# Every two weight slabs get places of their own for hi and lo within 256 bytes, in a one-core hybrid decoder layer

## The chip, the cores and the metric

The kernel runs on one core of a Trainium2 chip. The metric is the device time of one execution in microseconds (us), as the median of several runs.

## What is computed

One layer of a decoder trunk in float32 over 256 tokens of width 2048. An input projection (2048 to 6152 columns) feeds a gated causal convolution (31 taps, 8 channel groups) and a four-head mLSTM; their outputs go through an output projection (2048 to 2048), then a gated feed-forward part (2048 to 2 x 5632, a three-tap convolution on the gate, 5632 to 2048), with RMS norms around them. Cut to what matters:

```python
hn = rmsnorm(x, norm_mix_g);  p = hn @ w_in + b_in
u  = silu(group_norm(causal_dwconv(p[a] * sigmoid(p[g]), conv_dw_w, conv_dw_b), 8, gn_g, gn_b))
q, k = silu(causal_dwconv(p[q, k]));  v, o, li, lf = p[v], sigmoid(p[o]), p[i], log_sigmoid(p[f])
hm = group_norm(mlstm_chunkwise(q, k, v, li, lf), 4, mlstm_hn_g) * o
x  = x + concat(u, hm) @ w_out
up = rmsnorm(x, norm_ffn_g) @ w_up
x  = x + (silu(causal_dwconv(up[:5632])) * up[5632:]) @ w_down
out = rmsnorm(x, norm_final_g)
```

## The kernel before

All weights come as slabs of two row blocks of 128: 128 partitions by two times `w` float32 columns (`w` is 512, or 344 in the o projection). There are 400 slabs, in the order in which they are used, and one loop over them issues everything, by hand (`manual_schedule`). In turn i of the loop the SP queue is told to load slab i+5 (`load`, lines 178 to 193), slab i+3 is split (`split`, lines 195 to 224), and the matmuls of slab i are issued. A split is a rounding to float32r on ScalarE (`hi`, line 219) and the difference `raw - hi` on VectorE, or for some slabs on GpSimd (`lo`, line 224). hi and lo have four buffers each (`SPLIT_BUFS`), raw five. The other operand of each product is also kept as a high and a low part, and a product is the sum of three float32r matmuls (hi by high, hi by low, lo by high).

The stages, and in which role hi and lo stand in each:

- a and g columns of w_in, then later q and k columns (`ws_group`, line 254): hi and lo are the stationary operand (the weights that TensorE loads), the moving operand is a block of 256 columns of `xp`. 64 slabs, 24 matmuls each, 1536 matmuls of 256 columns.
- o columns (`xs_group`, lines 298 to 300, `w` = 344): hi and lo are the moving operand, the weights are 128 columns of `xp`. 24 slabs, 288 matmuls of 344 columns. The second row block of a slab begins 344 x 4 = 1376 bytes behind the first, which is 96 more within 256.
- v columns (the same lines, `w` = 512): 16 slabs, 192 matmuls of 512 columns, weights from `xp`.
- output projection (the same lines): 32 slabs, 384 matmuls of 512 columns, weights from `mixh` and `mixl`.
- w_up (`wp_group`, lines 279 and 280): hi and lo are the weights; a matmul with hi moves 512 columns of `x1p` (which lies where `xp` lay), one with lo moves 256. 176 slabs, 1408 matmuls of each kind. This stage is the longest.
- w_down (lines 298 to 300 for three column blocks, lines 850 to 852 in `down_last` for the last): hi and lo move, the weights are from `ah` and `al`. 88 slabs, 792 + 240 matmuls of 512 columns and 48 of 256.

Where the tiles lie, in bytes of a partition, modulo 256, by the layout of the built kernel: every buffer of hi and of lo begins at 160 (the buffers are 4096 bytes apart), `xp` and `x1p` at 192, and `mixh`, `mixl`, `ah` and `al` at 160. All offsets inside them that the matmuls use are multiples of 512 bytes, except the 1376 of the o projection. So the place of a slab tile less the place of its partner, modulo 256, is 224 against `xp` and `x1p` (64 for the second row block in the o projection), and 0 against `mixh`, `mixl`, `ah` and `al`. This difference is called the **distance** below.

Besides, seven little arrays of constants (biases, taps, gains: `load_rows`, lines 110 to 118) are loaded as rows into seven buffers of 512 bytes (tag `rows`), turned by TensorE in `transpose_rows` (line 154) and copied out. They are loaded at the start (G) and in turns 1, 3 and 5, and turned at the start and in turns 10 and 12. `mlstm_scores` (line 574) writes one tile of tag `pw`, 384 columns, for each of four heads, into four buffers.

Of the kernel before, what the change touches and what calls it, by code (L numbers as in the profile page):

```python
# [9 lines left out]
F32 = mybir.dt.float32  # L10
F32R = mybir.dt.float32r
# [4 lines left out]
P = 128  # L16
# [15 lines left out]
W = 512  # L32

RAW_BUFS = 5
SPLIT_BUFS = 4
AHEAD = 3
SIG = 4
WARM = (6, 5)
BY_K = 3


@with_exitstack
def hybrid_layer_kernel(
# [7 lines left out]
    act, dve, pool, pe = nc.scalar, nc.vector, nc.gpsimd, nc.tensor  # L51
# [4 lines left out]
    slab = ctx.enter_context(tc.tile_pool(name="slab", bufs=1))  # L56
    ps = ctx.enter_context(tc.tile_pool(name="ps", bufs=1, space=PSUM))
    inner = ExitStack()
    mid = inner.enter_context(tc.tile_pool(name="mid", bufs=1))
# [3 lines left out]
    def mm_bank(name):  # L63
        return ps.tile([P, 512], F32, tag="mm", name=name, bufs=4)
# [42 lines left out]
    warm = cst.tile([P, 1], F32, tag="warm", name="warm")  # L107
    act.copy(warm, ones[:, 0:1])

    def load_rows(parts, name):  # L110
        n = sum(p[1] for p in parts)
        r = mid.tile([P, P], F32, tag="rows", name="rows_" + name, bufs=7)
        o = 0
        for ap, k in parts:
            nc.sync.dma_start(r[o:o + k, :], ap)
            o += k
        return r, n
# [4 lines left out]
    rows = {}  # L122
# [44 lines left out]
    slabs = []  # L167
# [5 lines left out]
        tasks[cur[0] + delay].append((fn, cost))  # L173

    raw_t, hi_t, lo_t = {}, {}, {}
    mid_hook = []

    def load(i):
# [5 lines left out]
        if len(s["src"].shape) == 4:  # L184
            d = d.rearrange("p (k s c) -> p k s c", k=s["nk"], s=2)
            for h in range(2):
                if i < BY_K:
                    nc.sync.dma_start(d[:, h], s["src"][:, h])
# [11 lines left out]
    def split_tiles(i):  # L200
        s = slabs[i]
        n = s["nk"] * s["w"]
        raw = raw_t.pop(i)
        hi = slab.tile([P, 2 * W], F32R, tag="hi", name=f"hi{i}", bufs=SPLIT_BUFS)
        lo = slab.tile([P, 2 * W], F32R, tag="lo", name=f"lo{i}", bufs=SPLIT_BUFS)
        s["eng"] = pool if s["pool"] and i >= 8 and i % 2 else dve
        hi_t[i] = hi[:, :n].rearrange("p (k c) -> p k c", k=s["nk"])
        lo_t[i] = lo[:, :n].rearrange("p (k c) -> p k c", k=s["nk"])
        s["lo"] = 0.0 if s["eng"] is pool else 1.1 * n + 30
        return raw, hi, lo  # L210
# [15 lines left out]
    def w_slab(wap, kt, nk, col, w, fn, on_pool):  # L226
        if col is None:
            src = wap(kt)
        else:
            src = wap[kt * P:(kt + nk) * P, col:col + w].rearrange("(k p) c -> p k c", p=P)  # L230
        slabs.append(dict(src=src, w=w, nk=nk, mm=fn, pool=on_pool))


    def ws_group(wap, col, mov, nk, done, on_pool):
        st = {}

        def mk(kt):
            def fn(hi, lo):
                if kt == 0:
                    st["b"] = [mm_bank("ws0"), mm_bank("ws1")]  # L240
                mh, ml = mov()
                for k in range(2):
                    if mid_hook and mid_hook[0][0] == k:
                        mid_hook.pop(0)[1]()
                    hh, hl, lh = (hi, mh), (hi, ml), (lo, mh)
                    i = cur[0]
                    if i >= NK // 2:
                        steps = [(ct, a) for ct in range(4) for a in (hh, hl, lh)]
                    else:
                        steps = [(ct, a) for a in ((hh, lh, hl) if i + k == 0 else (hh, hl, lh)) for ct in range(4)]  # L250
                    for ct, (w, m) in steps:
                        o = v2(st["b"][ct // 2])[:, ct % 2, :]
                        first = kt + k == 0 and ct % 2 == 0 and w is hi and m is mh
                        pe.matmul(o, w[:, k, ct * P:(ct + 1) * P], m[:, kt + k, :], start=first,  # L254
                                  stop=kt + k == nk - 1 and w is lo, skip_group_check=True)
                if kt + 2 == nk:
                    done(st["b"])
            return fn

        for kt in range(0, nk, 2):  # L260
            w_slab(wap, kt, 2, col, W, mk(kt), on_pool)
# [3 lines left out]
    def wp_group(wap, col, done, alloc):  # L265
        st = {}

        def mk(kt):
            def fn(hi, lo):
                if kt == 0:  # L270
                    st["b"] = alloc()
                mp = xT["p2"]
                for k in range(2):
                    first, last = kt + k == 0, kt + k == NK - 1
                    m2 = mp[:, kt + k, :, :].rearrange("p h t -> p (h t)")
                    for ct in range(4):
                        o = st["b"][ct]
                        cs = slice(ct * P, (ct + 1) * P)
                        pe.matmul(o, hi[:, k, cs], m2, start=first, stop=last, skip_group_check=True)  # L279
                        pe.matmul(o[:, 0:T], lo[:, k, cs], mp[:, kt + k, 0, :], start=False, stop=last, skip_group_check=True)  # L280
                if kt + 2 == NK:
                    done(st["b"])
            return fn

        for kt in range(0, NK, 2):
            w_slab(wap, kt, 2, col, W, mk(kt), False)
# [18 lines left out]
    def xs_group(wap, col, w, stat, nk, done, on_pool):  # L305
        st = {}
        for kt in range(0, nk, 2):
            xs_slab(wap, col, w, stat, kt, kt == 0, kt + 2 == nk, st, done, on_pool)
# [39 lines left out]
    def done_ag(p):  # L348
        def fn(banks):
            sg = []  # L350

            def ev():
                for k in range(2):
                    c = 2 * p + k
                    act.activation(up[c][:, upos:], v2(banks[0])[:, k, :], AF.Identity, bias=bi[:, c:c + 1])
                sg.append(t2k("sg"))
                for k in range(2):
                    c = 2 * p + k
                    act.activation(v2(sg[0])[:, k, :], v2(banks[1])[:, k, :], AF.Sigmoid, bias=bi[:, 8 + c:9 + c])

            def mul():
                for k in range(2):
                    c = 2 * p + k
                    dve.tensor_mul(up[c][:, upos:], up[c][:, upos:], v2(sg[0])[:, k, :])
                conv_pair(p)
            d0 = 5 if p == 0 else 1
            after(d0, lambda: scale_banks(banks), 1300)
            after(d0 + 1, ev)
            after(d0 + 2, mul, 700)
        return fn  # L370
# [110 lines left out]
    def done_o(b):  # L481
        def fn(banks):
            def ev():
                for tt in range(NT):
                    dve.scalar_tensor_tensor(og[:, tt, b * OW:(b + 1) * OW], banks[tt][:, :OW], norm["r"][:, tt:tt + 1],
                                             bb[:, 1024 + b * OW:1024 + (b + 1) * OW], op0=ALU.mult, op1=ALU.add)

            def sig():
                n = OW if b < 2 else DC - 2 * OW
                for tt in range(NT):  # L490
                    o = og[:, tt, b * OW:b * OW + n]
                    act.activation(o, o, AF.Sigmoid)
                if b == 2:
                    gates()
            after(1, ev, 900)
            after(SIG, sig)
        return fn
# [65 lines left out]
    pw = {}  # L563
# [324 lines left out]


    ag = w_in[:, 0:2 * DC].rearrange("(k p) (s c) -> p k s c", p=P, s=2)  # L890
    for j in range(4):
        ws_group(lambda kt, j=j: ag[:, kt:kt + 2, :, T * j:T * (j + 1)], None, get_xT, NK, done_ag(j), True)
    for b in range(3):
        xs_group(w_in, OFF_O + OW * b, OW, get_xT, NK, done_o(b), True)
    for half in range(2):
        ws_group(w_in, OFF_Q + 512 * half, get_xT, NK, done_qk(0, half), True)
        ws_group(w_in, OFF_K + 512 * half, get_xT, NK, done_qk(1, half), True)

    at = defaultdict(list)
    v_start = len(slabs)  # L900
    for hp in range(2):
        xs_group(w_in, OFF_V + 512 * hp, W, get_xT, NK, done_v(hp), True)
    at[v_start - 2] += [(0, 0), (1, 1)]
# [3 lines left out]
        return mixh, mixl  # L907

    p3_start = len(slabs)
    sts = [{}, {}, {}, {"cv": True}]  # L910
    for n0 in (0, 2):
        for half in range(2):
            for n in (n0, n0 + 1):
                for kt in range(8 * half, 8 * half + 8, 2):
                    xs_slab(w_out, 512 * n, W, get_mix, kt, kt == 0, kt == 14, sts[n], done_out(n), False)

    for j in range(NF // 4):
        wp_group(w_up, 512 * j, done_gate(j), gate_banks)
        wp_group(w_up, DFF + 512 * j, done_up(j), up_banks)
    for n in range(3):  # L920
        xs_group(w_down, 512 * n, W, lambda: (ffn["ah"], ffn["al"]), NF, done_down(n, 512 * n, W), False)
    down_last(3, 1536, W, SPLIT_BUFS)
# [124 lines left out]
    credit = 0.0  # L1047
    split_next = [BY_K]
    for i in range(len(slabs)):
# [20 lines left out]
        while bg and credit > 0:  # L1070
            name = bg[0][0].__name__
            if name == "tail" and not first:
                break
            fn, cost = bg.popleft()
# [37 lines left out]
```

## Time and profile before

| | us |
|---|---|
| median of 3 runs | 1131.5 (1130.9 to 1131.64) |
| the profiled execution, its own time | 1131.08 |
| its span in the profile | 1129.3 |
| TensorE busy in it | 1118.7 |
| VectorE / ScalarE / GpSimd busy | 746.0 / 578.9 / 131.6 |

The profile calls TensorE's matmuls PE and its weight loads PEld, VectorE DVE, ScalarE ACT, GpSimd POOL and the DMA-issuing SyncE SP. A line such as L254 is a line of the kernel. The ends of matmuls are modelled and they overlap, so the duration of one matmul is no price; how far apart two of them start is one. Starts are given to 0.01 us, so the pitch (start to start) is read over many matmuls.

### The profile page before, as it was taken

The page shows a single profiled execution, that of the slowest core. Times are in us where ns is not written, and L with a number is a line of the kernel's source. Part 1 is how long each engine was busy: PE and PEld are TensorE (multiplying, and loading weights), DVE is VectorE, ACT ScalarE, POOL GpSimd, SP SyncE. Part 2 cuts the span into 40 slices and gives each one's busy share as a digit, 9 for nine tenths or more (in the row PEclk, how much of TensorE's full clock was granted, in tenths as well). Part 3 has the DMA queues.
Part 4 walks back from the last instruction along what each step waited for, and adds up shares of the span by engine and source line. Part 5 has one row for each costly group of instructions (what it writes and reads, how often), then busy time and mean ns, then how long its engine had stood idle before and what let it go on. Part 6 is the DMA issues. An engine that isn't in the chain of part 4 may idle for free.

```text
span 1129.3 us, 16955 instructions
## 1 busy us (share of the span) xinstructions
PE 1118.7 (99%) x6506; PEld 994.4 (88%) x6506; DVE 746.0 (66%) x1139; ACT 578.9 (51%) x823; POOL 131.6 (12%) x100
## 2 busy tenths in 40 slices
PE   9999999999999999999999999999999999999997
PEld 9999999998888888888888888888888888888886
DVE  5498999986765557657666666676576645454543
ACT  5745476754545455555545555455555444343433
POOL 0443554534200000000000000000000000000000
PEclk9999999999999999999999999999999999999999
DMA  8864665565655666666666666666666666666662
GB/s 262 272 190 125 193 205 186 175 183 166 218 192 184 173 195 190 192 188 185 188 199 191 184 191 189 194 188 192 188 186 188 197 193 230 197 188 196 191 195 89
DMA packets 122681, 215.40 MB, mean 191 GB/s; under 512 B 7440, under 2 KB 33256, under 8 KB 122088
## 3 DMA queue, kind: packets, MB, share of 16 engines
q1 hardware_dynamic: 121048, 209.92, 61.8%
q10 hardware_dynamic: 1552, 4.39, 1.0%
q8 instruction: 51, 0.84, 0.3%
q14 instruction: 30, 0.25, 0.1%
HBM read 212.19 MB, written 2.10 MB: 190 GB/s over the span
## 4 chain that ended last, share of the span: by engine, by line
PE 95%; DVE 3%; ACT 1%; issue 1%; DMA 0%; ACTq 0%; POOLq 0%; POOL 0%
PE ws L254 16%; PE gate L279 14%; PE up L279 14%; PE xs L298 9%; PE xs L299 9%; PE xs L300 9%; PE up L280 8%; PE gate L280 8%; PE xs L852 2%; PE xs L850 2%; PE xs L851 2%; DVE conv L386 2%; DVE lo L224 1%; DMA xs<-in_x_dram 0%; PE xT L940 0%
## 5 line engine op out<-in xcount | busy, mean ns | idle before, releaser
L224 DVE TENSOR_TENSOR lo<-raw,hi 128x1024 fp32r<-128x1024 f32 (+2 forms) x355 | 434.6, 1225 | 326.6 <-ACT hi L219 325.5
L219 ACT CAST hi<-raw 128x1024 fp32r<-128x1024 f32 (+2 forms) x401 | 411.5, 1030 | 452.4 <-PE xs L300 152.5
L279 PE MATMUL gate<-x1p,hi 128*128 128x512 f32 x704 | 245.0, 390 | 0.0
L279 PE MATMUL up<-x1p,hi 128*128 128x512 f32 x704 | 244.5, 390 | 0.0
L280 PE MATMUL up<-x1p,lo 128*128 128x256 f32 x704 | 198.5, 282 | 0.0
L280 PE MATMUL gate<-x1p,lo 128*128 128x256 f32 x704 | 198.5, 282 | 0.0
L254 PE MATMUL ws<-xp,hi 128*128 128x256 f32 x1024 | 178.5, 282 | 0.0
L279 PEld LDWEIGHTS up<-x1p,hi 128*128 128x128 f32 x704 | 132.2, 188 | 27.7
L279 PEld LDWEIGHTS gate<-x1p,hi 128*128 128x128 f32 x704 | 132.2, 188 | 27.6
L254 PEld LDWEIGHTS ws<-xp,hi 128*128 128x128 f32 x1024 | 153.4, 189 | 0.8 <-issue 0.3
L254 PE MATMUL ws<-xp,lo 128*128 128x256 f32 x512 | 135.5, 280 | 0.5 <-DVE lo L224 0.5
L280 PEld LDWEIGHTS gate<-x1p,lo 128*128 128x128 f32 x704 | 133.1, 189 | 0.0
L280 PEld LDWEIGHTS up<-x1p,lo 128*128 128x128 f32 x704 | 133.1, 189 | 0.0
L224 POOL TENSOR_TENSOR lo<-raw,hi 128x1024 fp32r<-128x1024 f32 (+1 forms) x48 | 111.1, 2317 | 148.2 <-ACT hi L219 142.2
L299 PE MATMUL xs<-lo,ah 128*128 128x512 f32 x264 | 102.7, 389 | 0.0
L300 PE MATMUL xs<-hi,al 128*128 128x512 f32 x264 | 102.7, 389 | 0.0
L298 PE MATMUL xs<-hi,ah 128*128 128x512 f32 x264 | 102.7, 389 | 0.0
L386 DVE SCALAR_TENSOR_TENSOR conv<-up,cB,conv 128x256 f32<-128x256 f32 x240 | 97.6, 478 | 0.0
L254 PEld LDWEIGHTS ws<-xp,lo 128*128 128x128 f32 x512 | 93.2, 189 | 0.9 <-DVE lo L224 0.7
L827 POOL TENSOR_TENSOR rf<-ms,halves 128x1 f32<-128x1 f32 x2 | 1.1, 550 | 711.7 <-DVE ms L821 711.7
L300 PEld LDWEIGHTS xs<-hi,al 128*128 128x128 f32 x264 | 49.6, 188 | 10.4
L298 PEld LDWEIGHTS xs<-hi,ah 128*128 128x128 f32 x264 | 49.6, 188 | 10.4
(186 smaller groups left out, 1204.5 us busy)
## 6 DMA issues: line engine op xcount, KB each, us to landing
raw<-in_w_up_dram SPq DMA_DIRECT2D x176, 512.0 KB, 3.9
raw<-in_w_down_dram SPq DMA_DIRECT2D x88, 512.0 KB, 4.7
raw<-in_w_in_dram SPq DMA_DIRECT2D x48, 512.0 KB, 4.4
raw<-in_w_in_dram SPq DMA_DIRECT2D x64, 256.0 KB, 4.6
raw<-in_w_out_dram SPq DMA_DIRECT2D x32, 512.0 KB, 4.6
raw<-in_w_in_dram SPq DMA_DIRECT2D x24, 344.0 KB, 3.4
x<-in_x_dram ACTq DMA_DIRECT2D x2, 1024.0 KB, 7.7
xs<-in_x_dram SPq DMA_DIRECT2D x7, 256.0 KB, 5.6
```

The costliest lines, as they stand in the source:

```text
L219: copy(hi[:, c], raw[:, c])
L224: slabs[i]["eng"].tensor_sub(lo[:, c], raw[:, c], hi[:, c].bitcast(F32))
L254: pe.matmul(o, w[:, k, ct * P:(ct + 1) * P], m[:, kt + k, :], start=first, stop=kt + k == nk - 1 and w is lo, skip_group_check=True)
L279: pe.matmul(o, hi[:, k, cs], m2, start=first, stop=last, skip_group_check=True)
L280: pe.matmul(o[:, 0:T], lo[:, k, cs], mp[:, kt + k, 0, :], start=False, stop=last, skip_group_check=True)
L298: pe.matmul(o, sh[:, kt + k, ts_], hi[:, k, :w], start=first and k == 0, stop=False)
L299: pe.matmul(o, sh[:, kt + k, ts_], lo[:, k, :w], start=False, stop=False)
L300: pe.matmul(o, sl[:, kt + k, ts_], hi[:, k, :w], start=False, stop=last and k == 1)
L386: dve.scalar_tensor_tensor(a, up[c][:, t:t + T], cB[:, 8 * t + c:8 * t + c + 1], a, op0=ALU.mult, op1=ALU.add)
L850: pe.matmul(o, sh[:, kt, ts_], hi[:, k, c:c + cw], start=kt == first, stop=False, skip_group_check=True)
L851: pe.matmul(o, sh[:, kt, ts_], lo[:, k, c:c + cw], start=False, stop=False, skip_group_check=True)
L852: pe.matmul(o, sl[:, kt, ts_], hi[:, k, c:c + cw], start=False, stop=kt == NF - 1, skip_group_check=True)
```

## The change

Each buffer of hi and lo is made 256 bytes longer (`ROOM` = 64 columns), and the 1024 columns that are used begin at an offset inside it that depends on the slab. `places` gives it: a list of pairs for hi and lo is set per stage by `new_stage`, and every two slabs take the next pair. `BASE` = 224 is the distance of the buffers' own start from `xp`, so that the numbers in a list are distances from `xp`; where the partner is `mixh`, `mixl`, `ah` or `al`, 32 is taken off, and they are distances from these. The lists: `Q_WS` (a and g, q and k, w_down) has for hi all eight multiples of 32 and for lo the same plus 0, 64, 128 or 192; `Q_XS` (o, v, output projection) has the sixteen pairs of multiples of 64; `Q_FFN` (w_up) has all 64 pairs of multiples of 32 and then 24 pairs in which lo stands at 16, 144, 80 or 208. The stages take from them: a and g 16 pairs, q and k the other 16, o 12, v 8, output projection 16, w_up all 88, w_down 44. To make room the rows of constants no longer have seven buffers of their own: three of them at a time are slices of a tile of tag `pw`, three such tiles in all. Number, order, shape and engine of all instructions stay as they are. The sizes of all the tiles that move are multiples of 256, so the other tiles keep their places within 256.

```diff
--- before.py
+++ after.py
@@ -37,6 +37,8 @@
 SIG = 4
 WARM = (6, 5)
 BY_K = 3
+ROOM = 64
+BASE = 224
 
 
 @with_exitstack
@@ -107,9 +109,14 @@
     warm = cst.tile([P, 1], F32, tag="warm", name="warm")
     act.copy(warm, ones[:, 0:1])
 
+    row_tiles = []
+
     def load_rows(parts, name):
         n = sum(p[1] for p in parts)
-        r = mid.tile([P, P], F32, tag="rows", name="rows_" + name, bufs=7)
+        if not row_tiles:
+            t = mid.tile([P, 384], F32, tag="pw", name="rows_" + name, bufs=4)
+            row_tiles.extend(t[:, c * P:(c + 1) * P] for c in (2, 1, 0))
+        r = row_tiles.pop()
         o = 0
         for ap, k in parts:
             nc.sync.dma_start(r[o:o + k, :], ap)
@@ -173,6 +180,23 @@
         tasks[cur[0] + delay].append((fn, cost))
 
     raw_t, hi_t, lo_t = {}, {}, {}
+    stage = {}
+
+
+    def places():
+        n = (len(slabs) - stage["at"]) // 2
+        q = stage["q"]
+        h, l = q[n % len(q)]
+        return (h - BASE) % 256 // 4, (l - BASE) % 256 // 4
+
+    def new_stage(q):
+        stage["at"], stage["q"] = len(slabs), q
+
+    Q8 = [32 * a for a in range(8)]
+    Q_FFN = [(a, b) for a in Q8 for b in Q8] + [(a, b) for a in (64, 192, 0, 128, 32, 224) for b in (16, 144, 80, 208)]
+    Q_WS = [(a, (a + b) % 256) for b in (0, 64, 128, 192) for a in Q8]
+    Q_XS = [(a, b) for a in (0, 64, 128, 192) for b in (0, 64, 128, 192)]
+
     mid_hook = []
 
     def load(i):
@@ -201,8 +225,9 @@
         s = slabs[i]
         n = s["nk"] * s["w"]
         raw = raw_t.pop(i)
-        hi = slab.tile([P, 2 * W], F32R, tag="hi", name=f"hi{i}", bufs=SPLIT_BUFS)
-        lo = slab.tile([P, 2 * W], F32R, tag="lo", name=f"lo{i}", bufs=SPLIT_BUFS)
+        hi = slab.tile([P, 2 * W + ROOM], F32R, tag="hi", name=f"hi{i}", bufs=SPLIT_BUFS)
+        lo = slab.tile([P, 2 * W + ROOM], F32R, tag="lo", name=f"lo{i}", bufs=SPLIT_BUFS)
+        hi, lo = (t[:, o:o + 2 * W] for t, o in zip((hi, lo), s["at"]))
         s["eng"] = pool if s["pool"] and i >= 8 and i % 2 else dve
         hi_t[i] = hi[:, :n].rearrange("p (k c) -> p k c", k=s["nk"])
         lo_t[i] = lo[:, :n].rearrange("p (k c) -> p k c", k=s["nk"])
@@ -228,7 +253,7 @@
             src = wap(kt)
         else:
             src = wap[kt * P:(kt + nk) * P, col:col + w].rearrange("(k p) c -> p k c", p=P)
-        slabs.append(dict(src=src, w=w, nk=nk, mm=fn, pool=on_pool))
+        slabs.append(dict(src=src, w=w, nk=nk, mm=fn, pool=on_pool, at=places()))
 
 
     def ws_group(wap, col, mov, nk, done, on_pool):
@@ -888,16 +913,20 @@
 
 
     ag = w_in[:, 0:2 * DC].rearrange("(k p) (s c) -> p k s c", p=P, s=2)
+    new_stage(Q_WS)
     for j in range(4):
         ws_group(lambda kt, j=j: ag[:, kt:kt + 2, :, T * j:T * (j + 1)], None, get_xT, NK, done_ag(j), True)
+    new_stage(Q_XS)
     for b in range(3):
         xs_group(w_in, OFF_O + OW * b, OW, get_xT, NK, done_o(b), True)
+    new_stage(Q_WS[16:] + Q_WS[:16])
     for half in range(2):
         ws_group(w_in, OFF_Q + 512 * half, get_xT, NK, done_qk(0, half), True)
         ws_group(w_in, OFF_K + 512 * half, get_xT, NK, done_qk(1, half), True)
 
     at = defaultdict(list)
     v_start = len(slabs)
+    new_stage(Q_XS)
     for hp in range(2):
         xs_group(w_in, OFF_V + 512 * hp, W, get_xT, NK, done_v(hp), True)
     at[v_start - 2] += [(0, 0), (1, 1)]
@@ -907,6 +936,7 @@
         return mixh, mixl
 
     p3_start = len(slabs)
+    new_stage([(a - 32, b - 32) for a, b in Q_XS])
     sts = [{}, {}, {}, {"cv": True}]
     for n0 in (0, 2):
         for half in range(2):
@@ -914,9 +944,11 @@
                 for kt in range(8 * half, 8 * half + 8, 2):
                     xs_slab(w_out, 512 * n, W, get_mix, kt, kt == 0, kt == 14, sts[n], done_out(n), False)
 
+    new_stage(Q_FFN)
     for j in range(NF // 4):
         wp_group(w_up, 512 * j, done_gate(j), gate_banks)
         wp_group(w_up, DFF + 512 * j, done_up(j), up_banks)
+    new_stage([(a - 32, b - 32) for a, b in Q_WS])
     for n in range(3):
         xs_group(w_down, 512 * n, W, lambda: (ffn["ah"], ffn["al"]), NF, done_down(n, 512 * n, W), False)
     down_last(3, 1536, W, SPLIT_BUFS)
```

## Rows read from the trace of the kernel before

**Rows 1.** page, part 1: busy time and instructions; part 2: granted clock

```profile
PE 1118.7 (99%) x6506; PEld 994.4 (88%) x6506; DVE 746.0 (66%) x1139; ACT 578.9 (51%) x823; POOL 131.6 (12%) x100
...
PEclk9999999999999999999999999999999999999999
```

**Rows 2.** page, part 4: the chain, by engine

```profile
PE 95%; DVE 3%; ACT 1%; issue 1%; DMA 0%; ACTq 0%; POOLq 0%; POOL 0%
```

**Rows 3.** waits of TensorE: us in total, times, longest

```profile
PE warm L968 <- POOL ident masks.py:199: 1.4, 1, 1.4
...
PE xT L940 <- DMA xs<-in_x_dram: 0.5, 1, 0.5
...
PE ws L254 <- DVE lo L224: 0.5, 1, 0.5
...
PE xs L299 <- DVE lo L224: 0.4, 1, 0.4
```

**Rows 4.** chain in order of time, ws stages: start us, us, what

```profile
55.99 24.03 PE ws L254 x204
...
243.16 2.80 PE ws L254 x24
```

**Rows 5.** timeline of TensorE, o projection, first and last: start us, us, engine, line

```profile
118.06 0.32 PE L298 MATMUL xs<-hi,xp 128*128 128x344 f32 x1
...
142.41 0.32 PE L298 MATMUL xs<-hi,xp 128*128 128x344 f32 x1
```

**Rows 6.** timeline of TensorE, v projection, first and last

```profile
250.60 0.40 PE L298 MATMUL xs<-hi,xp 128*128 128x512 f32 x1
...
268.80 0.40 PE L298 MATMUL xs<-hi,xp 128*128 128x512 f32 x1
```

**Rows 7.** timeline of TensorE, w_up, first and last

```profile
500.07 0.39 PE L279 MATMUL gate<-x1p,hi 128*128 128x512 f32 x1
...
516.02 0.39 PE L279 MATMUL up<-x1p,hi 128*128 128x512 f32 x1
```

**Rows 8.** timeline of TensorE, output projection, first and last

```profile
360.05 0.39 PE L298 MATMUL xs<-hi,mixh 128*128 128x512 f32 x1
...
383.85 0.39 PE L298 MATMUL xs<-hi,mixh 128*128 128x512 f32 x1
```

**Rows 9.** timeline of TensorE, w_down, 512 columns and then 256

```profile
1100.04 0.39 PE L850 MATMUL xs<-hi,ah 128*128 128x512 f32 x1
...
1115.46 0.39 PE L852 MATMUL xs<-hi,al 128*128 128x512 f32 x1
...
1115.68 0.28 PE L850 MATMUL xs<-hi,ah 128*128 128x256 f32 x1
...
1118.56 0.28 PE L850 MATMUL xs<-hi,ah 128*128 128x256 f32 x1
```

**Rows 10.** chain in order of time, mLSTM scores, plain float32 passes

```profile
241.85 0.86 PE S L570 x4
```

**Rows 11.** busy time by stretch: us, PE, PEld, DVE, ACT, POOL, PEclk, DMA

```profile
150.00:200.00 50.00, 50.00 (x413) 48.51 (x414) 49.17 (x95) 35.19 (x49) 26.32 (x14) 1.00 0.60 190
...
500.00:600.00 100.00, 100.00 (x579) 88.67 (x578) 66.11 (x89) 52.26 (x77) 0.00 (x0) 1.00 0.66 190
...
600.00:700.00 100.00, 100.00 (x579) 88.63 (x578) 68.55 (x95) 54.22 (x81) 0.00 (x0) 1.00 0.66 190
```

**Rows 12.** groups by line and shape, the splits: busy us, mean ns, idle before

```profile
L224 DVE TENSOR_TENSOR lo<-raw,hi 128x1024 fp32r<-128x1024 f32 x337 | 417.3, 1239 | 322.3 <-ACT hi L219 321.3
...
L219 ACT CAST hi<-raw 128x1024 fp32r<-128x1024 f32 x373 | 391.1, 1051 | 434.9 <-PE xs L300 143.0 <-PE gate L279 114.9 <-PE up L279 91.2
```

**Rows 13.** rows of constants turned, scores written: ns, first and last start

```profile
L154 PE MATMUL tr<-ident,rows_G x1: 285/285/285, 2.9 to 2.9; 16*128 16x16 f32 x1
...
L154 PE MATMUL tr<-ident,rows_D x2: 237/240/242, 48.1 to 48.2; 88*128 88x88 f32 x2
...
L574 DVE SCALAR_TENSOR_TENSOR pw<-S,wt x4: 557/558/559, 243.2 to 285.2; 128x384 f32<-128x384 f32 x4
```

## The prediction, made before the change was run

> **What bounds the kernel now.** I read the page's first two parts first: TensorE is busy 1118.7 of 1129.3 us, and the granted clock is at its upper level, 2.4 GHz, throughout [rows 1]. The chain that ended last is 95% TensorE [rows 2], and all its waits for data together are 2.8 us, nearly half of that before the first product [rows 3]. So it is not starved: what it costs is how far apart its matmuls start. A busy TensorE says nothing about that, so I went on to the pitch, stage by stage, from long runs of matmuls without a break. Only pitches that lie on both sides of a change in roles or places can tell what this change does.
>
> A matmul of n columns that took one column per cycle at 2.4 GHz would take n / 2.4 ns. What a matmul takes beyond that I call its **extra**:
> - a, g, q and k: 24 matmuls in 2.80 us are 116.7 ns each against 106.7, so 10.0 extra; in an earlier stretch 204 in 24.03 us, 117.8 each, 11.1 extra [rows 4]. Distance 224, slab tiles are the weights. I take 10.5.
> - o: 156 starts from the first to the last row, 156.1 ns against 143.3: 12.8 [rows 5]. Distance 224 and 64 in turn, slab tiles move.
> - v: 78 starts, 233.3 against 213.3: 20.0 [rows 6]. Distance 224, slab tiles move.
> - w_up: 92 starts, 173.4 on the mean of 512 and 256 columns (160.0): 13.4 [rows 7]. Distance 224, slab tiles are the weights.
> - output projection: 105 starts, 226.7 against 213.3: 13.4 [rows 8]. Distance 0, slab tiles move.
> - w_down: 68 starts, 226.8, so 13.5; with 256 columns 24 starts, 120.0, so 13.3 [rows 9]. Distance 0, slab tiles move.
>
> Two things are to be seen. The extra is the same for 256 and for 512 columns at the same places [rows 9], so it is paid once a matmul and weight load, not per column. And it differs between v and w_down, which have the same shape, the same engine and the same role of the slab, by 6.5 ns [rows 6, 9]; what differs is the partner's tile and with it the distance. The plain float32 passes of the scores, 4 in 0.86 us, take 215 ns for 256 columns, twice the columns' time of the float32r ones (213.3) with 1.7 ns left over [rows 10]. So most of the extra is not a fixed price of a matmul either: where the moving operand is read at half the pace, it is gone. My reading is that weight load and moving operand get in each other's way in SBUF, and that it depends on where both stand. That other engines' traffic is not the cause: the splits run in bursts all through w_up, and two stretches with different DVE and ACT busy time hold the same 579 matmuls in 100 us [rows 11].
>
> In all the extra is 1536 x 10.5 + 288 x 12.8 + 192 x 20.0 + 2816 x 13.4 + 384 x 13.4 + 1080 x 13.5 ns = 16.1 + 3.7 + 3.8 + 37.7 + 5.1 + 14.6 = 81 us. This is all that a change of places can act on.
>
> **The change, part by part.** *The rows of constants.* G is turned at 2.9 us and the last two tiles by 48.2; the first score is written into a `pw` tile at 243.2 [rows 13]. No reader of a row comes within 190 us of the tile's next writer; the loads keep their order on SP and their bytes. If the loads of A and B1, which share G's tile, had to wait for G's turning, that lies before turn 1, in which the first of them is issued. Cost 0, with that cover; without it one of TensorE's turns would be late by a load, and nothing but `cA` to `cD` behind it.
>
> *The splits.* ScalarE and VectorE write to and read from shifted places, 373 casts of 1051 ns and 337 differences of 1239 ns, with 435 and 322 us of idle time ahead of them [rows 12]. If a place made them 10% slower (no row shows one that does), w_up's VectorE would go from 66% to about 70% busy [rows 11] and TensorE would not see it. The exception is q and k, where VectorE is busy 49.2 of 50 us [rows 11]: there 10% on some 25 splits, 3 us, would reach the end. I take 0, keep 0 to +3.
>
> *The pitch.* This is the sum. Distance is now scanned, so each stage gets the mean over its list instead of its one value. The rows show six readings, 10.5, 12.8, 20.0, 13.4, 13.4 and 13.5; their mean is 13.9. For a place that no row shows I take that mean, an estimate; its bounds are 10.0 and 20.0, the best and the worst reading.
> - a, g, q, k: from the best reading to the mean, 3.4 x 1536 = +5.2 us.
> - w_up: 0.5 x 2816 = +1.4 us.
> - v: its list has multiples of 64 only, and here 0 and 64 for hi, so the nearest rows are the 13.4 of distance 0 [rows 8]: -6.6 x 192 = -1.3 us.
> - o: in the new list as in the old one row block is a multiple of 64 away and the other is 32 off that: 0.
> - output projection +0.5 x 384 = +0.2, w_down +0.4 x 1080 = +0.4 us.
> - w_up's lo at 16, 144, 80 or 208: 24 pairs, so 48 slabs of 8 weight loads, 384 loads; bounds -3.4 to +6.6 ns each, -1.3 to +2.5 us; I take the middle, +0.6.
>
> Sum +6.5 us, on 1131.08 of the profiled execution (its span and 1.8 around it): 1137.6. The runs' median is 0.4 above the profiled one, so **1138**.
>
> *Bounds.* With every matmul at 10.0: -0.8 - 0.8 - 1.9 - 9.6 - 1.3 - 3.8 = -18 us. With all at 20.0: 14.6 + 2.1 + 0 + 18.6 + 2.5 + 7.0 = +45. A list that goes round all distances reaches neither end; the mean would have to lie a half of the way to the one (-9) or to the other (+22).
>
> The Trainium skill speaks against any effect: "TensorE: Matmul & The Clock Gate", section "Step-by-step: what each phase is for", says that the moving operand and the weight load have a read port each and that loading the next weights takes no bandwidth from the running matmul. "SBUF — State Buffer", section "Who interferes with whom", adds that PE never waits on anyone. By that the sum is 0 and the time 1131.5. The trace does not agree, with 233.3 against 226.8 ns for the same 512 columns.
>
> **The rivals.**
> - *The mean is better than the places before.* Distance 224 and 0, on which nearly all the time rests, were worse than the typical place. For it: v shows that a distance can cost 6.5 ns, so one may also save it, and the scores' 1.7 ns show that little is fixed. Against it: the largest stage sits at 13.4, under the mean of the readings, and a and g at the lowest. If the mean were 11.7, half way from 13.4 to 10.0: -1.7 x 2816 - 1.8 x 1080 - 1.7 x 384 + 1.2 x 1536 - 8.3 x 192 - 1.1 x 288 ns = -7.4 us, so 1124. In q and k a gain would be cut by VectorE.
> - *Places do not matter, roles do.* v would be slow because it takes its weights from `xp` and moves the slab, whatever the distance. Then nothing changes: 1131.5. For it: w_up holds the same 579 in both stretches [rows 11] though its tiles go round four buffers each; but these all have the same place within 256, so that is weak. Against it: o has the roles of v and 12.8 against 20.0; what differs, besides 344 columns, is that half of its distances are 64.
> - *Places in which both reads stay in step.* The slower end: weight loads that begin near the moving operand's place may be held over and over, as in v. The price is v's 20.0 or more. If every second place of all lists had it, and the others what their stage has now: half of the +45, 1154. It decides the result as soon as more than a tenth of the places are like v (+4.5). A time far above the forecast is this one.
> - *The shift does not do what it says*, because the period is not 256 bytes: with a shorter one of 64 or 128 some pairs repeat and the mean is taken over fewer places, the same forecast; with a longer one the 4352 bytes between buffers add places that no row shows. It widens the range, no more.
>
> **How the numbers follow.** The forecast, slower by a mean near that of the readings (1133.8 to about 1147), 0.50; in step, above that, 0.09; places do not matter, or the parts cancel (within 2.3 us), 0.16; the mean is better, 0.25. A measurement of this kernel can tell about 0.2% from no change, 2.3 us. So slower 0.59, same 0.16, faster 0.25. The range leaves out one in ten on either side: low end -9 us, a mean half way to the best reading, 1122; high end 1153, half way to the worst. The forecast's own part of it is 1134 to 1147.
>
> **What would show it.** The number of matmuls and their columns stay, so TensorE's pitch by pairs of slabs tells all: in w_up, 32 matmuls to two slabs at 13.4 extra are 5.55 us, and this should now change every two slabs, in steps that come back with the list. If all pairs take the same, places do not matter and the second rival is right. v should come down to about 227 ns a matmul; if it stays at 233, its role and not its distance makes it slow, and that step is wrong. a, g, q and k should rise above 117.8 ns. If waits of TensorE for hi or lo appear in q and k, the step on the splits was wrong; waits for rows of constants ahead of 50 us would make the first step wrong. If w_up's mean pitch falls under 173.4, the forecast's sign is wrong.

## The result and the profile after

The changed kernel takes **1141.17 us** (median of 3 runs, 1140.8 to 1141.5) against 1131.5: 9.7 us more, a ratio of 1.0087 with a 95% interval of 1.0064 to 1.011. The profiled execution has a time of its own of 1141.5 us and a span of 1139.8.

The page of the changed kernel, busy time and instructions, granted clock, and the first line of the chain:

```profile
PE 1128.5 (99%) x6506; PEld 992.1 (87%) x6506; DVE 741.7 (65%) x1139; ACT 578.7 (51%) x823; POOL 132.3 (12%) x100
...
PEclk9999999999999999999999999999999999999999
...
PE 93%; DMA 3%; DVE 1%; ACT 1%; issue 1%; SPq 1%; POOL 0%; ACTq 0%; POOLq 0%; DVEq 0%
```

(In the chain, "issue" is time in which an engine waited for nothing that the profile shows, and a q behind the name of an engine is its sequencer.) Same number of instructions, same granted clock, still a chain of TensorE [rows 1, 2]. TensorE is busy 9.8 us longer, and the span grew by 10.5. TensorE's waits for data in the changed kernel (us in total, times, longest) come to 3.6 us against 2.8 before [rows 3], all ahead of 120 us:

```profile
PE warm L1000 <- POOL ident masks.py:199: 1.4, 1, 1.4
PE ws L279 <- POOL lo L249: 0.9, 1, 0.9
PE xT L972 <- DMA xs<-in_x_dram: 0.6, 1, 0.6
PE rsb L365 <- ACT dg L360: 0.5, 1, 0.5
PE xs L324 <- DVE lo L249: 0.2, 1, 0.2
```

The waits are 0.8 us longer, so nearly all of the loss is pitch. It shows in the busy table by stretch (us, PE busy with the number of matmuls, granted clock, DMA share, GB/s); the first stretch is w_up, the second w_down. First the kernel before:

```profile
410.00:620.00 210.00, 210.00 (x1214) 1.00 0.66 190
...
900.00:1040.00 140.00, 140.00 (x620) 1.00 0.63 201
```

and the changed kernel:

```profile
410.00:620.00 210.00, 210.00 (x1205) 1.00 0.66 190
...
900.00:1040.00 140.00, 140.00 (x604) 1.00 0.62 197
```

w_up loses 9 of 1214 matmuls in equal time, w_down 16 of 620: the heavier loss is where the forecast saw almost none. By stages, from the first matmul of each to the first of the next in the two traces (w_down to the end of its last), with the extra as the mean over a stage's matmuls that follow another without a break:

| stage | before, us | after, us | difference | forecast | extra before, ns | extra after, ns |
|---|---|---|---|---|---|---|
| a, g | 96.64 | 97.72 | +1.1 | +5.2 with q, k | 10.7 | 11.3 |
| q, k | 98.07 | 97.79 | -0.3 | in the row above | 10.1 | 11.1 |
| o | 46.55 | 46.59 | 0.0 | 0 | 13.0 | 13.9 |
| v | 51.71 | 51.31 | -0.4 | -1.3 | 19.7 | 17.5 |
| output projection | 93.53 | 94.98 | +1.5 | +0.2 | 13.9 | 17.9 |
| w_up | 489.49 | 492.61 | +3.1 | +2.0 | 13.4 | 14.5 |
| w_down | 239.84 | 245.52 | +5.7 | +0.4 | 13.3 | 18.6 |
| sum | | | +10.7 | +6.5 | | |

**Pair by pair.** The timeline of TensorE shows the lists at work. In w_up of the changed kernel (start us, us, engine, line), the first matmul of the pair (64, 0), of (64, 32), of (64, 64) and of the pair that follows, 32 matmuls apart:

```profile
484.62 0.39 PE L304 MATMUL gate<-x1p,hi 128*128 128x512 f32 x1
...
490.06 0.40 PE L304 MATMUL gate<-x1p,hi 128*128 128x512 f32 x1
...
495.61 0.39 PE L304 MATMUL gate<-x1p,hi 128*128 128x512 f32 x1
...
501.25 0.40 PE L304 MATMUL gate<-x1p,hi 128*128 128x512 f32 x1
```

5.44, 5.55 and 5.64 us are 170.0, 173.4 and 176.3 ns a matmul: extras of 10.0, 13.4 and 16.3 with the same instructions. In w_down, the second slab of the pair (0, 0), which is 12 matmuls, and then the pairs (32, 32), (64, 64) and (96, 96) of 24 each:

```profile
889.30 0.39 PE L323 MATMUL xs<-hi,ah 128*128 128x512 f32 x1
...
892.02 0.40 PE L323 MATMUL xs<-hi,ah 128*128 128x512 f32 x1
...
897.63 0.40 PE L323 MATMUL xs<-hi,ah 128*128 128x512 f32 x1
...
903.13 0.40 PE L323 MATMUL xs<-hi,ah 128*128 128x512 f32 x1
...
908.74 0.40 PE L323 MATMUL xs<-hi,ah 128*128 128x512 f32 x1
```

226.7, 233.8, 229.2 and 233.8 ns: extras of 13.3, 20.4, 15.8 and 20.4. The distance of before, (0, 0), is by far the best of the four. Worked out in this way for all pairs: in w_down the 42 pairs ahead of its last four slabs, whose matmuls stand in another order, lie between 14.4 and 20.8, and 22 of them at 19.5 or more; in w_up the 88 pairs lie between 10.0 and 16.8; in the output projection between 14.7 (13.3 once settled, again at (0, 0)) and 20.0; in a, g, q and k between 6.7 and 14.2.

### The profile page after: what moved, and what is told of

The parts are those of the page before. It is cut to its first block, busy times and chain, and to the rows that moved or that the text cites. A ratio compares the mean times of both kernels' runs of the same rounds, so it can differ in the third digit from the quotient of the medians.

```text
span 1139.8 us, 16957 instructions
## 1 busy us (share of the span) xinstructions
PE 1128.5 (99%) x6506; PEld 992.1 (87%) x6506; DVE 741.7 (65%) x1139; ACT 578.7 (51%) x823; POOL 132.3 (12%) x100
## 4 chain that ended last, share of the span: by engine, by line
PE 93%; DMA 3%; DVE 1%; ACT 1%; issue 1%; SPq 1%; POOL 0%; ACTq 0%; POOLq 0%; DVEq 0%
PE gate L304 14%; PE up L304 14%; PE ws L279 12%; PE xs L324 10%; PE xs L323 10%; PE xs L325 10%; PE up L305 7%; PE gate L305 7%; PE xs L877 2%; PE xs L875 2%; PE xs L876 2%; DMA raw<-in_w_in_dram 2%; DMA bb<-in_b_in_dram 1%; DVE conv L411 1%; DMA xs<-in_x_dram 0%
## 5 line engine op out<-in xcount | busy, mean ns | idle before, releaser
L323 PEld LDWEIGHTS xs<-hi,ah 128*128 128x128 f32 x264 | 49.6, 188 | 11.6
```

The costliest lines, as they stand in the source:

```text
L323: pe.matmul(o, sh[:, kt + k, ts_], hi[:, k, :w], start=first and k == 0, stop=False)
```

## The experiments

Four questions: does anything but the places cost time; is it the distance or the slab's own place; which stages carry the loss; and does a pair's reading in the scan hold when a whole stage stands there. All are the changed kernel with other lists; two also move `xp` and `x1p`. A pair is one of `new_stage`, first hi, then lo; (224, 224) puts a slab at offset 0 of its buffer, its place of before.

### 1. All lists fixed at the places of before

```diff
 # the same in all seven calls of new_stage
-    new_stage(Q_WS)
+    new_stage([(224, 224)])
```

> The changed kernel with every slab at the places of before (distance 224 from xp, 0 from the mix and act tiles), so that only the longer buffers and the rows of constants in the pw tiles are left of the change. Theory of the places: the whole 9.7 us are the pitch of the matmuls at the scanned places, so this gives 1131.5, at most 1.5 off, with an extra of 10 to 11 ns in a, g, q and k, 20 in v, 13.4 in w_up and in w_down. Rival: the rows or the longer buffers carry a part (the waits of TensorE before 50 us are longer in the changed kernel's trace, 3.6 us against 2.8): 1133 to 1136, with waits ahead of the first 50 us.

Measured: 1131.33 us, 1.000 of before (0.9990 to 1.0009). Its pitch is back too (the two stretches of w_up and w_down):

```profile
410.00:620.00 210.00, 210.00 (x1215) 1.00 0.66 190
900.00:1040.00 140.00, 140.00 (x619) 1.00 0.63 202
```

What follows: the rows of constants in the score tiles' buffers and the longer buffers cost nothing that this run can tell, which is about 1 us. TensorE's waits come to 4.5 us here, against 2.8 [rows 3], and still the time is that of before. The 9.7 us are the places.

### 2. The slab's own place moved together with xp and x1p

```diff
+XO = 8
-    xT["p"] = cst.tile([P, NK, 2, T], F32R, tag="xp", name="xp")
+    xT["p"] = cst.tile([P, NK * 2 * T + 64], F32R, tag="xp", name="xp")[:, XO:XO + NK * 2 * T].rearrange("p (k h t) -> p k h t", k=NK, h=2)
 # the same for x1p; lists: (0, 0) in the five stages up to w_up without the output projection, (224, 224) in the others
```

> hi, lo, xp and x1p all moved by 32 bytes (192 and 224 instead of 160 and 192), distance as before. Theory that the distance counts: all extras as before, 1131.5. Rival, that each tile's own place within a line of 64 bytes counts: hi and lo now stand on a multiple of 64 and xp does not, the other way round than before; w_up and v would leave 13.4 and 20.0 by a nanosecond or more each, over 2.8 us in the sum.

Measured: 1131.19 us, 1.0002 of before (0.9992 to 1.0011), and every stage has the extra of before: a and g 10.8, q and k 10.3, v 20.0, w_up and w_down 13.3. Moving both sides by 32 bytes, the one common shift that was tried, changes nothing.

### 3. Only xp and x1p moved: distance 64 with the slabs where they were

```diff
+XO = 40
 # the tiles of xp and x1p as in experiment 2; all lists (224, 224)
```

> hi and lo at the places of before (160 within 256), but xp and x1p moved from 192 to 96, so that the distance is 64 for both (o: 64 and 160). Theory that the distance counts: the extras of the changed kernel at 64, 64: 7.3 in a, g, q and k (10.4 before), 15.6 in v (20), 16.7 in w_up (13.4), w_down unchanged at 13.4; sum -4.8 - 0.8 + 9.3 = +3.7, 1135. Rival, that the place of hi and lo alone counts: nothing changes there, 13.4 in w_up and 20 in v, 1131.5.

`xp` and `x1p` now begin at 96 within 256, the slabs still at 160. Measured: 1135.82 us, 1.0043 of before (1.0028 to 1.0058). The stretch of w_up, and a piece of q and k from the chain in order of time (start us, us, what):

```profile
410.00:620.00 210.00, 210.00 (x1191) 1.00 0.66 188
```

```profile
170.83 10.90 PE ws L280 x96
```

The same 96 matmuls in the kernel before, and then in the changed one:

```profile
173.46 11.21 PE ws L254 x96
```

```profile
173.45 11.50 PE ws L279 x96
```

10.90 us are 113.5 ns each, an extra of 6.9. The slabs' own places are untouched, and still a, g, q and k went from 10.4 to 7.0, v from 19.7 to 16.2, w_up from 13.4 to 16.7; w_down, whose partners did not move, stayed at 13.3. It is the distance that counts, as the two scans also say by themselves: v (partner `xp`) and the output projection (partner `mixh`, `mixl`) went through the same first eight pairs of `Q_XS`, and seven of the eight have the same extra within 0.7 ns in both, from 15 to 20. The eighth, (64, 64), has 15.4 in v and 20.0 in the output projection; experiment 4 shows that one distance can have two values, but not that this is the reason here.

### 4. Each stage fixed at what looked like the best pair of the scan

```diff
-    new_stage(Q_WS)          # a, g, and the same for q, k, there Q_WS[16:] + Q_WS[:16]
+    new_stage([(192, 64)])
-    new_stage(Q_XS)          # v
+    new_stage([(0, 0)])
-    new_stage(Q_FFN)         # w_up
+    new_stage([(64, 0)])
 # o, output projection, w_down: (224, 224)
```

> Each stage fixed at the place with the smallest extra in the changed kernel's trace: a, g, q, k at hi 192, lo 64 (6.7 ns there, 10.4 before), v at 0, 0 (13.3 in the second slab of the pair, 20 before), w_up at 64, 0 (10.2, 13.4 before), o, output projection and w_down as before. Theory of the places: what a pair of slabs shows holds for a whole stage, so -3.7 x 1536, -6.5 x 192 and -3.2 x 2816 ns: -5.7 - 1.2 - 9.0 = -15.9, 1115.6. Rival: VectorE, busy 49.2 of 50 us between 150 and 200 us before, becomes the bound in q and k: its 2.8 us don't come, 1118.5, with waits of TensorE for lo. Rival: a low extra is an accident of two slabs after a change of places and does not last: nothing gained, 1130 to 1132.

Measured: 1133.9 us, 1.0023 of before (1.0013 to 1.0034). This missed by 18 us, with the wrong sign; the second rival, that a low extra does not last, came nearest. v did what it should (stage 50.77 us, down 0.9) and a and g came to 7.1. But w_up, at the very pair that had 10.0 in the scan, ran at 15.0 for nearly the whole stage. TensorE's timeline near its start:

```profile
399.84 0.40 PE L304 MATMUL gate<-x1p,hi 128*128 128x512 f32 x1
...
407.27 0.40 PE L304 MATMUL gate<-x1p,hi 128*128 128x512 f32 x1
...
407.62 0.60 PE L365 MATMUL rsb<-dg,ones 128*128 128x128 f32 x4
...
409.11 0.40 PE L304 MATMUL gate<-x1p,hi 128*128 128x512 f32 x1
...
413.66 0.39 PE L304 MATMUL up<-x1p,hi 128*128 128x512 f32 x1
```

From 399.84 to 407.27 are 42 matmuls of 176.9 ns, extra 16.9; then four small matmuls of another kind come in between; from 409.11 to 413.66 are 26 of 175.0, extra 15.0, and that held for all the slabs up to the end of the stage. Nothing about the places within 256 changed at 407.6 us. The same is to be seen in q and k of this kernel, all at one place:

```profile
203.56 10.89 PE ws L279 x96
...
214.88 25.68 PE ws L279 x216
```

113.4 and 118.9 ns, extras of 6.8 and 12.2, a few microseconds apart. VectorE, the first rival, is not what holds q and k back here: the one wait of TensorE for a lo in that stage is 0.5 us, as before [rows 3], and in experiment 3 the stage took 94.72 us against 98.07 before. My reading is that a distance does not have one pitch but a few repeating patterns of starts, that the way in which TensorE came there decides which of them holds, and that it can last until other work comes between; experiment 6 tests this. The rows of before may show the same, taken there for spread: 117.8 and 116.7 ns in the same roles at the same distance [rows 4].

### 5. The changed kernel with output projection and w_down put back

```diff
-    new_stage([(a - 32, b - 32) for a, b in Q_XS])   # output projection
+    new_stage([(224, 224)])
-    new_stage([(a - 32, b - 32) for a, b in Q_WS])   # w_down
+    new_stage([(224, 224)])
```

> The changed kernel with the output projection and w_down put back to distance 0 and all other lists kept. By the stages of the changed kernel's trace these two carry 1.5 + 5.7 = 7.2 of the 9.7 us (they took 278.5 us from the first matmul of the output projection to the last of w_down without w_up, against 273.1 and 60.3 + 179.5 + 93.5 before): 1134.0, with an extra of 13.3 to 13.4 in both, and w_up at 14.5 as in the changed kernel. Rival: the loss is spread over the stages as forecast, most of it in a, g, q and k; then this gives 1140.

Measured: 1134.1 us, 1.0026 of before (1.0016 to 1.0037). 7.1 of the 9.7 us are these two stages, as the table of stages has it (1.5 + 5.7); the rival's 1140 is out.

### 6. w_up at (64, 0), with one pair at (32, 224) in its middle

```diff
-    new_stage(Q_FFN)
+    new_stage([(64, 0)] * 44 + [(32, 224)] + [(64, 0)] * 43)
 # all other lists (224, 224)
```

> All stages at the places of before, but w_up at 64, 0, with one pair at 32, 224 in the middle (slabs 224 and 225 of 136 to 311). Theory of the pattern: at 64, 0 there are several repeating patterns of starts, and which one holds depends on how the stage came there; the waits for the first x1p blocks throw it into the slow one (15.0 ns) and it stays to the middle, and after 32, 224, as in the changed kernel, the fast one follows (10.0) and stays to the end: 1408 x 1.6 - 1376 x 3.4 ns = -2.4 us, 1129. Rival, that 10.0 there was a matter of the first slabs after any change of place or that the place has drifted to its one value: 15.0 in both halves, +4.5 us, 1136.

Measured: 1128.85 us, 0.9981 of before (0.9972 to 0.9990). (32, 224) is the pair that stands ahead of (64, 0) in `Q_FFN`: from it the scan had come to the fast pattern. TensorE's timeline around it:

```profile
638.64 0.39 PE L304 MATMUL gate<-x1p,hi 128*128 128x512 f32 x1
...
640.04 0.39 PE L304 MATMUL up<-x1p,hi 128*128 128x512 f32 x1
...
645.59 0.39 PE L304 MATMUL up<-x1p,hi 128*128 128x512 f32 x1
...
646.95 0.39 PE L304 MATMUL up<-x1p,hi 128*128 128x512 f32 x1
```

8 matmuls in 1.40 us at (64, 0), 32 in 5.55 at (32, 224), 8 in 1.36 at (64, 0) again: extras of 15.0, 13.4 and 10.0. The stretches on either side of it:

```profile
410.00:620.00 210.00, 210.00 (x1204) 1.00 0.65 189
660.00:870.00 210.00, 210.00 (x1238) 1.00 0.66 193
```

34 more matmuls in the same 210 us, at the same places, with nearly the same share of DMA beside them. That the stage would have changed there by itself is ruled out by experiment 4, which had (64, 0) throughout and no pair elsewhere; its second stretch:

```profile
660.00:870.00 210.00, 210.00 (x1202) 1.00 0.65 188
```

It is shown by this that a pattern, and not the place alone, sets the pitch.

### 7 and 8. A kernel made from this, and the same without its w_up part

```diff
-    new_stage(Q_WS)          # a, g, and the same for q, k
+    new_stage([(64, 64)])
-    new_stage(Q_XS)          # v
+    new_stage([(0, 0)])
-    new_stage(Q_FFN)         # w_up; in the second kernel [(224, 224)]
+    new_stage([(224, 224)] * 8 + [(32, 224)] + [(64, 0)] * 79)
 # o, output projection, w_down: (224, 224)
```

> A version made from the readings: a, g, q, k at 64, 64 (6.7 to 7.3 in all runs that had it), v at 0, 0 (13.3 after ten matmuls), o, output projection and w_down as before, w_up at 224, 224 for the 16 slabs in which TensorE still waits for x1p, then one pair at 32, 224, then 64, 0 to the end. Theory of the pattern: q and k -3.3 us, a and g -0.5 to -2, v -1, w_up -3.4 x 2528 = -8.6: 1116 to 1118. Rival: w_up falls into 15.0 after all, +4.0 instead: 1130.

Measured: **1119.56 us**, 0.990 of before (0.9884 to 0.9917): 11.6 us faster than the kernel before and 21.6 faster than the changed one.

> As the version made from the readings, but w_up wholly at the place of before (13.4). a, g, q, k at 64, 64 and v at 0, 0 are left: -0.5 to -2, -3.3, -1: 1125 to 1126.5. Rival, that TensorE's gain in a, g, q, k is given back in waits for splits or loads: 1129 to 1131, with waits of TensorE well above 2.8 us.

Measured: 1127.82 us, 0.9975 of before (0.9966 to 0.9984). The difference of the two, 8.3 us, is w_up: 481.06 against 489.48 us, extra 10.0 from its tenth pair of slabs to the end. The page of the faster kernel, and its w_up and w_down stretches:

```profile
PE 1104.8 (99%) x6506; PEld 980.5 (88%) x6506; DVE 746.1 (67%) x1139; ACT 577.7 (52%) x823; POOL 132.0 (12%) x100
```

```profile
410.00:620.00 210.00, 210.00 (x1234) 1.00 0.67 193
...
900.00:1040.00 140.00, 140.00 (x619) 1.00 0.63 201
```

The w_up stretch of the kernel without that part, for comparison:

```profile
410.00:620.00 210.00, 210.00 (x1214) 1.00 0.66 191
```

Both end 1.3 to 1.6 us above the upper end of what was expected. By stages the shortfall is in q and k, 1.2 and 0.4 us shorter instead of 3.3: they took a slow pattern for some time here too (in the faster kernel 11.1 in slabs 58 to 63, then mostly 6.7; in the other twice). The o stage, at its places of before, became 0.5 and 0.6 us longer. The rival of the last expectation came true in part: TensorE's waits come to 5.1 and 4.8 us against 2.8 [rows 3]. The two longest of the faster kernel after its first product:

```profile
PE ws L279 <- POOL lo L249: 1.3, 1, 1.3
PE xs L324 <- DVE lo L249: 0.9, 1, 0.9
```

a and g gained what was expected, 1.1 and 1.3 us, but not what their pitch alone would give: 7.1 instead of 10.7 is 2.8 us in 768 matmuls. The chain of the faster kernel in order of time:

```profile
29.37 7.24 DMA bb<-in_b_in_dram
36.63 5.97 DMA raw<-in_w_in_dram
...
45.18 0.78 PE rsb L365 x4
45.96 2.74 PE ws L279 x24
```

Ahead of 46 us the chain stands on loads: a faster TensorE has to wait for them. That point was reached at 45.45 us in the kernel before, whose chain is TensorE from 5.46 us up to there, and at 45.96 here.

## Why the prediction was right in its direction and not in its terms

Slower, and 1141.2 in the range of 1122 to 1153: the forecast of 1138 named the right mechanism with 6.5 of the 9.7 us. By its steps:

- *TensorE's pitch is what can change, and distance within 256 bytes is what changes it.* Held: experiments 2 and 3. The Trainium skill's rule, "TensorE: Matmul & The Clock Gate", section "Step-by-step: what each phase is for", by which weight load and moving operand have a port each and loading the next weights takes nothing from the running matmul, would leave the time at 1131.5. The runs do not agree: they show extras from 6.7 to 20.8 ns, which change with the distance of just these two operands. That they meet in SBUF, as I read it, no run shows.
- *The rows of constants cost 0.* Held within 1 us: experiment 1.
- *The splits cost 0.* Held: VectorE is busy 741.7 us against 746.0 [rows 1], and no wait for hi or lo appears in q and k.
- *An unseen place costs the mean of the six readings, 13.9.* This is the step that failed. The six came from stages with different roles and column counts, and I pooled them as if they were six draws from one list. They are not. The scans have a mean of 11.2 with 256 columns (a, g, q, k), 13.9 with 344 (o), and with 512 columns 17.5 (v), 17.9 (output projection) and 18.9 (w_down). w_up, which alternates 512 and 256, has 14.5: from the start of a matmul of 512 columns to the next start the extra is 18.0, from one of 256 it is 10.9. So the level goes with the columns, though in w_up the slab is loaded and in w_down it moves. Seen against its own list, w_down's 13.5 was the best place of all, v's 20.0 an ordinary bad one, and a and g's 10.5 close to the mean.
- *The extra is the same for 256 and for 512 columns, so it is paid once a matmul.* This fell too, and the pooling rests on it: it was read at the one distance (0, 0) [rows 9]. The last four slabs of w_down in the changed kernel stand at (64, 128) and (96, 160), and each pair has 12 matmuls of 512 columns and later 12 of 256, in the same roles (first starts):

```profile
1120.61 0.39 PE L875 MATMUL xs<-hi,ah 128*128 128x512 f32 x1
...
1123.38 0.40 PE L875 MATMUL xs<-hi,ah 128*128 128x512 f32 x1
...
1126.19 0.28 PE L875 MATMUL xs<-hi,ah 128*128 128x256 f32 x1
...
1127.61 0.28 PE L875 MATMUL xs<-hi,ah 128*128 128x256 f32 x1
...
1129.05 0.28 PE L875 MATMUL xs<-hi,ah 128*128 128x256 f32 x1
```

These are about 231, 234, 118 and 120 ns a matmul: extras of about 18 and 20 with 512 columns, and of about 12 and 13 with 256, at the same two pairs of places.

- The terms follow. w_down and output projection: forecast +0.6, measured +7.2, of which w_down's is 5.25 ns on 1080 matmuls. a, g, q, k: forecast +5.2, measured +0.8 (about +1.2 by the pitch alone). The first is 6.6 us short and the second 4.4 too high; that they largely cancel is luck, and the reason why the total looks better than its parts. w_up: forecast +2.0 (0.2 of it counts the 384 loads of lo twice), measured +3.1, the one term about right in size; its pairs with lo at 16, 80, 144 and 208 are no worse than the others (14.0 against 14.6). v: forecast -1.3, measured -0.4, since only one of its eight pairs, (0, 0), has the 13.3 that I took for all of them. o: 0 and 0.
- *The rivals.* "Places do not matter, roles do" fell by experiment 3, in which roles stayed and pitches moved; that stages of different kind have different levels was true, and it was what the forecast lacked, but the level goes with the columns; whether the role adds to it is not shown. "The mean is better" fell for these lists, though better places exist. "In step" had the size right in w_down, where half of the pairs pay what v paid, and was wrong about w_up, where none comes near it. "The period is not 256": buffers of one tag now lie 4352 bytes apart, which alternates the place within 512, and experiment 1, which has these buffers, has the pitch of before in w_up and w_down; so nothing longer is needed. A period of 128 would make (0, 0) and (128, 128) alike, and in w_down's scan they have 14.4 to 15.0 and 20.0.

The a and g stage is no evidence for either side. Experiment 1, with the places of before, has 97.29 us there, between before's 96.64 and the changed kernel's 97.72. In the traces of experiment 1 and of the changed kernel TensorE came to its second group of transposes earlier (6.93 and 7.21 us against 8.48), and then had to wait for a lo from GpSimd (1.3 and 0.9 us), which it did not before. In the kernel before, its first matmuls of 256 columns stand 213 ns apart up to that point, in the other two mostly 118; the granted clock in the rows is 1.00 there in all three, and the reason is not shown.

What stays open: what makes the extra, why it is larger with more columns, and what picks the pattern. The distance is counted from the partner to the slab, so between loaded and moving operand it has opposite signs in w_up and in w_down; the two were not compared at the same sign. Places of hi off the multiples of 32 bytes were not tried, nor a common shift other than 32, nor other pairs to switch w_up over in its first slabs.

## What to carry to other kernels

When TensorE is busy 99% and waits for nothing, read its pitch stage by stage and subtract the columns' time: here 81 us of 1131 lay there, and 11.6 of them came back by choosing where tiles stand within 256 bytes, with no instruction changed. Judge a stage's place only against other places of the same role and number of columns, and try a place on the whole stage before trusting a reading of a few slabs. A list that goes round all places gives every stage its mean, so it is a way to measure, and a loss for every stage that already stands well.

## What the runs showed of the hardware that was not expected

- At one distance the starts settle into one of a few repeating patterns: w_up at (64, 0) ran at extras of 16.9, 15.0 and 10.0, q and k at (192, 64) at 6.8 and 12.2. One pattern held for 168 slabs (2,688 matmuls) without a change, with the other engines at work beside it (w_up of experiment 4, 15.0). In experiment 6 the same pattern gave way to that of 10.0 after one pair of slabs elsewhere; in experiment 4 the pitch changed across four small matmuls of another kind, from 16.9 to 15.0 in w_up and from 6.8 to 12.2 in q and k.
- Long settled stretches come back to a few extras: 6.7, 10.0 and 11.1 ns with 256 columns (a, g, q, k), 13.3 and 20.0 with 512 (w_down, v), 10.0, 13.3 and 15.0 as the mean of both in w_up.
- Over a scan of places the extra is larger with more columns: 11.2 ns with 256, 13.9 with 344, 17.5 to 18.9 with 512. At the one distance (0, 0) it is the same, 13.3, for 256 and for 512.
- The best pitch seen with a weight load for each matmul is 113.4 ns for 256 columns, 6.7 over the columns' time; the worst pair, in w_down, paid 20.8.
